# Where the low parts are subtracted: GpSimd or VectorE ahead of the attention

## The chip, the cores and the metric

The kernel runs on one core of one Trainium2 chip. The metric is the device time in microseconds of one execution: the median of three executions, with the lowest and the highest beside it. The profile below is one further execution, taken by the hardware profiler; its own time is given with it.

## What is computed

One layer of a diffusion backbone over 1024 latent tokens of width 1024, with 256 context tokens as a prefix, all in float32. Cut to what matters:

```
h, hc = modulate(x), modulate(ctx)                      # RMSNorm, then scale and shift from c
q, k, v, hy, gates = split(h @ w_in + b_in)             # 8 query heads, 2 key/value heads of 128
kc, vc = the k and v columns for the context tokens
attn = softmax(rope(norm(q)) @ [kc; rope(norm(k))]^T) @ [vc; v]
K    = rfft(filter MLP over positions)                  # 2 orders x 512 channels, length 2048
hy_o = two gated long convolutions of dwconv3(hy) by K  # each irfft(rfft(u) * K)
x   += g1 * ((sig(ga) * (attn @ w_attn) + sig(gh) * (hy_o @ w_hy)) @ w_o + b_o)
x   += g2 * ((gelu(a) * g) @ w_down + b_down),  [a, g] = dwconv3(modulate(x) @ w_up + b_up)
out  = rmsnorm(x)
```

## The kernel before

Every large product is made of three TensorE passes over float32r operands (`mm3`, L184 to L186). An operand X is split into a high part, which is X cast to float32r by ScalarE, and a low part, which is X minus the high part: one subtraction of 128x512 elements in most places, through the helper `sub` (L174). The low part is needed by the second or the third pass. `sub` takes an engine, VectorE (`V`) unless it is told GpSimd (`G`).

The work up to the attention runs in this order of the program. The times are those of the profiled execution.

- To about 51 us: the small filter network and the modulation vectors.
- 51 to 152 us: the context tokens and the latent tokens are normalised, transposed and split into `hTh`, `hTl` by `norm_in` (L574 to L598), in pairs of 128-row tiles; beside it the filters' transforms run as a background generator (`filters`, with `split`, L388, for its 16-point DFT outputs `X`).
- 152 to 354 us: six weight chunks of `w_in` give the Hyena streams (`proj_ch`, then `hy_post`), with the filters' transforms still in the background, and `other_tables` (L720 to L734) makes high and low parts of ten transform tables: a load into `traw`, a cast into `thi`, a subtraction into `tlo`, two stores. `traw`, `thi` and `tlo` have one buffer each, so a table's load waits for the subtraction of the table before.
- 354 to 759 us: six gate chunks and six q, k, v chunks alternate (`gate_chunk`, `qkv_chunk`), with both long convolutions in the background (`longconv`: a forward transform to `zp`, the product with the filter, an inverse transform to `vp`, then `idft16` on VectorE). The transform tables `ft` and `it` come by DMA. `norm_rope` normalises and rotates q and k, and TensorE transposes the result.
- 759 to 860 us: two more gate chunks beside the first scores; `parts` (L1015) splits v, k and q for the attention.

Each weight chunk comes through `load_w` (L486): four times a load of 128x512 into `raw` (3 buffers), a cast into `whi` (6 buffers, ScalarE), and a subtraction into `wlo` (6 buffers). A third `raw` tile is reused only when the subtraction that reads it is done; the load that reuses it stands in SyncE's queue, and in the same queue stand the loads of the transform tables behind it. A `whi` or `wlo` buffer is reused when TensorE has finished with it.

Five calls place the subtraction on GpSimd: `load_w` by default (`wlo`), every second pair in `norm_in` (`hTl`), slots 5 and 7 of the filters' `split` (`Xl`), `other_tables` (`tlo`), and three of the `parts` calls (two of `v`, one of `kT`). After the attention `load_w` serves `w_hy` and `w_attn` as well. GpSimd's other work in the whole kernel is the low parts of q, the normalisation of the attention output and sums of down-projection weights during the attention, and low parts for `w_o`.

Order: up to the FFN the order on each engine is made by the planner of the tile framework, which goes by the order of the program and by its own estimates of when operands are ready; each engine then works its queue in order. From the FFN on (`tc.manual_schedule`) the order is written out by hand.

Of the kernel before, what the change touches and what calls it, by code (L numbers as in the profile page):

```python
# [165 lines left out]
def build(tc, A, out, stop=99):  # L166
# [6 lines left out]
    def sub(out, a, b, eng=V):  # L173
        eng.tensor_tensor(out=out, in0=a, in1=b, op=ALU.subtract)  # L174
# [220 lines left out]
    def filters():  # L395
        for half in range(2):
            for order in range(2):
                for kind in range(2):
                    z = fp.tile([P, 8, 256], F32, name="z", tag="z")
                    c0 = order * 512 + half * 256  # L400
                    wh = fp.tile([P, 256], F32R, name="woh", tag="woh")
                    S.copy(out=wh, in_=wo[:, kind, c0:c0 + 256])
                    wl = fp.tile([P, 256], F32R, name="wol", tag="wol")
                    sub(wl, wo[:, kind, c0:c0 + 256], wh)
                    for a2 in range(4):
                        if order == kind == 0:
                            decs[a2] = fp.tile([P, 2, 256], F32, name="dec", tag=f"dec{a2}")
                            ld(out=decs[a2], in_=A["k_dec"][half][:, a2 * 512:a2 * 512 + 512].rearrange(
                                "p (a c) -> p a c", a=2))
                        ps = pfh.tile([P, 2, 256], F32, name="fh", tag="fh")  # L410
                        for k in range(2):
                            a = 2 * a2 + k
                            T.matmul(ps[:, k], hms[:, a * P:a * P + P], wh, start=True, stop=False)
                            T.matmul(ps[:, k], hms[:, a * P:a * P + P], wl, start=False, stop=True)
                        tt(z[:, 2 * a2:2 * a2 + 2], ps, decs[a2], ALU.mult)
                    if kind == 0:
                        skip = fp.tile([1, 256], F32, name="skip", tag="ks", bufs=2)
                        ld(out=skip, in_=A["rows"][3:4, c0:c0 + 256])
                        tt(z[0:1, 0], z[0:1, 0], skip, ALU.add)
                    yield  # L420
                    def forward(slot, Xh, Xl):
                        tb = fwd_tab(slot)
                        ps = pfk.tile([P, 2, 256], F32, name="fk", tag="fk")
                        if slot == 0:
                            m = (0, 1) if kind == 0 else (2, 3)
                        else:
                            m = (0, 1) if kind == 0 else (1, 0)
                        mm3(ps[:, 0], *tb[m[0]], Xh[:, 0], Xl[:, 0], True, False)
                        mm3(ps[:, 0], *tb[m[1]], Xh[:, 1], Xl[:, 1], False, True)
                        if slot == 0:  # L430
                            ks = fp.tile([P, 256], F32, name="ks", tag="ks", bufs=2)
                            S.copy(out=ks, in_=ps[:, 0])
                            if kind == 0:
                                (rh, rl) = tb[2]
                                mm3(ps[0:1, 1], rh[:, 0:1], rl[:, 0:1], Xh[:, 0], Xl[:, 0], True, True)
                                st(out=k_d[order, half, :, 0], in_=ks)
                                kd = fp.tile([P, 256], F32, name="ks", tag="ks", bufs=2)
                                S.copy(out=kd, in_=ps[:, 0])
                                S.copy(out=kd[0:1], in_=ps[0:1, 1])
                                st(out=k_d[order, half, :, 1], in_=kd)  # L440
                            else:
                                V.memset(ks[0:1], 0.0)
                                ld(out=k_d[order, half, :, 2], in_=ks)
                        else:
                            ks = fp.tile([P, 256], F32, name="ks", tag="ks", bufs=2)
                            S.copy(out=ks, in_=ps[:, 0])
                            st(out=k_d[order, half, :, 1 + 2 * slot + kind], in_=ks)

                    ahead = []
                    for slot, X in dft16(fp, z, 2, kind == 0):  # L450
                        ahead.append((slot, *split(fp, X, 2, "X", G if slot in (5, 7) else V)))
                        yield
                        if len(ahead) > 1:
                            forward(*ahead.pop(0))
                            yield
                    forward(*ahead.pop(0))
                    yield
# [25 lines left out]
    def raw_tile():  # L483
        return wp.tile([P, 512], F32, name="raw", tag="raw", bufs=3)

    def load_w(src, pool=None, eng=G, nraw=3, nhi=6):  # L486

        pl = pool or wp
        res = []
        for i in range(len(src) if isinstance(src, list) else src.shape[0]):  # L490
            if isinstance(src, list):
                raw = src[i]
            else:
                raw = pl.tile([P, 2, 256], F32, name="raw", tag="raw", bufs=nraw)
                ld(out=raw, in_=src[i].rearrange("p (k c) -> p k c", k=2))
            hi = pl.tile([P, 2, 256], F32R, name="whi", tag="whi", bufs=nhi)
            S.copy(out=hi, in_=raw)  # L497
            lo = pl.tile([P, 2, 256], F32R, name="wlo", tag="wlo", bufs=nhi)
            sub(lo, raw, hi, eng)
            for k in range(2):  # L500
                res.append((hi[:, k], lo[:, k]))
        return res
# [72 lines left out]
    def norm_in(xs, r, s, c0, late=False):  # L575

        for i in range(2):
            V.tensor_scalar(out=xs[i], in0=xs[i], scalar1=r[:, i:i + 1], scalar2=None, op0=ALU.mult)
        hh, hl, cs = hTh[c0 // 512], hTl[c0 // 512], slice(c0 % 512, c0 % 512 + 256)
        for c0_ in range(0, KT, 2):  # L580
            if late:
                ps = ptr.tile([P, 2, 256], F32, name="tr", tag="tr")
            elif c0_ % 4 == 0:
                ps = pmm.tile([P, 4, 256], F32, name="mm", tag="mm")
            n = ps.shape[1]
            hf = hfp.tile([P, 2, 256], F32, name="hf", tag="hf")
            for c in (c0_, c0_ + 1):
                for i in range(2):
                    T.transpose(ps[:, c % n, i * P:(i + 1) * P], xs[i][:, c * P:(c + 1) * P], ident)
            for j in range(2):  # L590
                c = c0_ + j
                a_, b_ = mod1[:, 8 + c, s:s + 1], mod1[:, c, s:s + 1]
                if j == 0:
                    S.activation(out=hf[:, j], in_=ps[:, c % n], func=AF.Identity, scale=a_, bias=b_)
                else:
                    V.tensor_scalar(out=hf[:, j], in0=ps[:, c % n], scalar1=a_, scalar2=b_, op0=ALU.mult, op1=ALU.add)
            S.copy(out=hh[:, c0_:c0_ + 2, cs], in_=hf)
            sub(hl[:, c0_:c0_ + 2, cs], hf, hh[:, c0_:c0_ + 2, cs], (G, V)[c0_ // 2 % 2])  # L598


    def qk_pool(n):
# [118 lines left out]
    def other_tables():  # L720
# [4 lines left out]
        for src, dst, n in inv_r:  # L725
            raw = hyp.tile([P, 512], F32, name="traw", tag="traw", bufs=1)[:, 0:n * P]
            ld(out=raw, in_=src)
            hi = hyp.tile([P, 512], F32R, name="thi", tag="thi", bufs=1)[:, 0:n * P]
            S.copy(out=hi, in_=raw)
            lo = hyp.tile([P, 512], F32R, name="tlo", tag="tlo", bufs=1)[:, 0:n * P]  # L730
            sub(lo, raw, hi, G)
            st(out=dst[:, 0], in_=B32(hi).rearrange("p (a b) -> p a b", b=P))
            ld(out=dst[:, 1], in_=B32(lo).rearrange("p (a b) -> p a b", b=P))
            yield  # L734
# [291 lines left out]
    def pt_tile(odd=1):  # L1026
        return (ap if odd else pte).tile([P, NKEY], F32, name="Pt", tag="Pt", bufs=4)
# [3 lines left out]
    parts(kT[0], kT_d[0], pt_tile())  # L1031
    for i in range(2):
        parts([v[:, 5 * i:5 * i + 5] for v in vv], v_d[:, 5 * i:5 * i + 5],
              pt_tile().rearrange("p (k d) -> p k d", d=256), G)
    parts(kT[1], kT_d[1], pt_tile(), G)
    KS = ((1024, 256), (0, 512), (512, 512))

    def scores(q, g, qt, sm, Pt):
# [201 lines left out]
        return ps  # L1240

    for ci in range(4):
        w = load_w(A["w_hy"][ci], wp, nraw=5) if ci else load_w([raw_hy[:, 0], raw_hy[:, 1]], wp, V, nraw=5)
        for m2 in range(2):
            m = 2 * ci + m2
            ps = branch(w, m2, 4, hyh, hyl)
# [12 lines left out]

    mix = [half_pair(0), half_pair(1)]  # L1260
    for ci in range(4):
        w = load_w(A["w_attn"][ci], wp, nraw=5)
        for m2 in range(2):
            m = 2 * ci + m2
            ps = branch(w, m2, 8, *[[o[:, :, 512 * h:512 * h + 512] for h in range(2)] for o in (oTh, oTl)])
# [608 lines left out]
```

## Time and profile before

| | |
|---|---|
| median of 3 executions | 2023.29 us (2020.77 to 2024.64) |
| profiled execution, its time | 2025.56 us |
| its span, first to last instruction | 2023.8 us |
| TensorE matmul busy | 1893.8 us, 94% |
| VectorE busy | 1545.9 us, 76% |
| ScalarE busy | 968.2 us, 48% |
| GpSimd busy | 422.0 us, 21% |

An engine's busy time is the union of its instructions' spans. Idle time before an instruction is put down to what released it, by semaphore events. The profile also tells the clock that TensorE was granted, as a share of its full speed. In the stretches of the change, 51 to 860 us, GpSimd has 155 instructions; from the end of the attention's neighbourhood on, the change touches nothing.

### The profile page before, as it was taken

What the parts mean: (1) busy time and instruction counts of PE and PEld (TensorE: products, weight loads), DVE (VectorE), ACT (ScalarE), POOL (GpSimd) and SP (SyncE); (2) the same over time, 40 slices, a digit from 0 to 9 for tenths busy, and PEclk for the clock granted to TensorE, in tenths of its full rate; (3) what the DMA queues carried; (4) which work ended last, traced back from release to release, by engine and by line L of the source; (5) the groups of instructions that cost most, each with busy time, mean ns of one, the idle gap of its engine ahead of it and who ended that gap; (6) DMA issues with size and microseconds to landing.
All of it is one profiled execution on the core that took longest, in us unless ns stands there. A gap on an engine that the chain in (4) does not pass through costs nothing.

```text
span 2023.8 us, 27726 instructions
## 1 busy us (share of the span) xinstructions
PE 1893.8 (94%) x9776; PEld 1570.5 (78%) x9776; DVE 1545.9 (76%) x2630; ACT 968.2 (48%) x1958; POOL 422.0 (21%) x270
## 2 busy tenths in 40 slices
PE   7789899889989989999999999998999999899997
PEld 1667778879878888788887777787888888678885
DVE  6987885896878633677776663889888888878788
ACT  3754443442444334687777332345444444445443
POOL 0553331222141231344532133440000000000000
PEclk8899999999999999999999999999999999999998
DMA  7435434747555331444434874742333333349762
GB/s 296 158 102 201 150 97 156 243 145 240 185 168 158 126 130 58 135 141 150 128 100 85 287 273 168 253 151 65 120 108 106 115 104 109 126 149 339 249 204 98
DMA packets 181131, 322.54 MB, mean 159 GB/s; under 512 B 26955, under 2 KB 65359, under 8 KB 180096
## 3 DMA queue, kind: packets, MB, share of 16 engines
q1 hardware_dynamic: 156256, 287.01, 43.7%
q10 hardware_dynamic: 24736, 33.76, 4.7%
q8 instruction: 77, 1.26, 0.3%
q14 instruction: 62, 0.51, 0.1%
HBM read 245.03 MB, written 75.68 MB: 158 GB/s over the span
## 4 chain that ended last, share of the span: by engine, by line
PE 57%; DVE 21%; DMA 6%; issue 5%; ACT 3%; POOL 2%; SPq 0%; ACTq 0%; DVEq 0%; POOLq 0%
PE mm L186 6%; PE mm L185 6%; PE mm L184 6%; PE b L184 5%; PE b L186 5%; PE b L185 5%; PE tp L1144 3%; DVE ua L180 2%; DVE ug L180 2%; PE s L184 2%; PE s L186 2%; PE s L185 2%; PE o L185 2%; PE o L186 2%; PE o L184 2%
## 5 line engine op out<-in xcount | busy, mean ns | idle before, releaser
L174 POOL TENSOR_TENSOR wlo<-raw,whi 128x512 fp32r<-128x512 f32 x138 | 234.2, 1709 | 601.1 <-ACT whi L497 499.1
L184 PE MATMUL mm<-hTh,whi 128*128 128x512 f32 x448 | 180.5, 403 | 2.6 <-ACT sg L973 1.4
L185 PE MATMUL mm<-hTl,whi 128*128 128x512 f32 x448 | 179.8, 401 | 0.5 <-DVE hTl L174 0.5
L186 PE MATMUL mm<-hTh,wlo 128*128 128x512 f32 x448 | 179.4, 400 | 0.0
L1046 DVE TENSOR_REDUCE mx<-s 128x1 f32<-128x512 f32 (+1 forms) x192 | 113.3, 598 | 58.7 <-PE s L186 57.0
L185 PE MATMUL mm<-wlo,hTh 128*128 128x256 f32 x416 | 118.8, 286 | 8.8 <-POOL wlo L174 8.4
L1051 ACT ACTIVATE Pt<-s,mx 128x512 f32<-128x512 f32 (+1 forms) x192 | 116.1, 614 | 20.2 <-DVE mx L1049 18.8
L186 PE MATMUL mm<-whi,hTl 128*128 128x256 f32 x416 | 118.6, 285 | 0.7 <-DVE hTl L174 0.5
L174 DVE TENSOR_TENSOR PTl<-tp,PTh 128x512 fp32r<-128x512 f32 x160 | 108.2, 685 | 13.7 <-ACT PTh L1146 10.3
L184 PE MATMUL mm<-whi,hTh 128*128 128x256 f32 x416 | 118.5, 285 | 0.0
L388 ACT CAST Xh<-X 128x512 fp32r<-128x512 f32 x128 | 78.0, 620 | 76.1 <-DVE X L177 35.6
L1146 ACT CAST PTh<-tp 128x512 fp32r<-128x512 f32 x160 | 92.7, 594 | 39.5 <-PE tp L1144 39.4
L186 PE MATMUL b<-bh,al 128*128 128x512 f32 x284 | 110.6, 390 | 0.6 <-DVE al L174 0.6
L184 PE MATMUL b<-bh,ah 128*128 128x512 f32 x284 | 110.6, 390 | 0.4 <-ACT ah L1731 0.4
L185 PE MATMUL b<-bl,ah 128*128 128x512 f32 x284 | 110.6, 389 | 0.0
L497 ACT CAST whi<-raw 128x512 fp32r<-128x512 f32 x110 | 66.5, 617 | 87.7 <-PE mm L185 41.2
L174 DVE TENSOR_TENSOR Xl<-X,Xh 128x512 fp32r<-128x512 f32 x112 | 80.6, 737 | 35.2 <-ACT Xh L388 35.0
L184 PEld LDWEIGHTS mm<-hTh,whi 128*128 128x128 f32 x448 | 85.9, 192 | 18.5 <-ACT sg L973 1.8
L186 PEld LDWEIGHTS mm<-hTh,wlo 128*128 128x128 f32 x448 | 86.2, 192 | 16.3
L185 PEld LDWEIGHTS mm<-hTl,whi 128*128 128x128 f32 x448 | 86.3, 193 | 16.0 <-DVE hTl L174 0.9
L1144 PEld LDWEIGHTS tp<-ident,Pt 128*128 128x128 f32 x640 | 77.3, 140 | 22.7 <-issue 3.7
L1144 PE MATMUL tp<-ident,Pt 128*128 128x128 f32 x640 | 93.8, 273 | 1.1 <-DVE PTl L174 0.8
(388 smaller groups left out, 5770.4 us busy)
## 6 DMA issues: line engine op xcount, KB each, us to landing
raw<-w_up SPq DMA_DIRECT2D x132, 256.0 KB, 2.8
raw<-w_in SPq DMA_DIRECT2D x88, 256.0 KB, 3.1
wm<-w_mod SPq DMA_DIRECT2D x64, 256.0 KB, 4.3
raw<-act_d SPq DMA_DIRECT2D x25, 512.0 KB, 3.3
wd<-w_down SPq DMA_DIRECT2D x44, 256.0 KB, 4.2
ws_d<-wd SPq DMA_DIRECT2D x44, 256.0 KB, 4.4
act_d<-ug SPq DMA_DIRECT2D x44, 256.0 KB, 2.2
ft<-fwd_d SPq DMA_DIRECT2D x28, 384.0 KB, 4.0
```

The lines of the kernel that those rows point to most:

```text
L174: eng.tensor_tensor(out=out, in0=a, in1=b, op=ALU.subtract)
L180: eng.scalar_tensor_tensor(out=out, in0=a, scalar=s, in1=b, op0=op0, op1=op1)
L184: T.matmul(o, lh, rh, start=start, stop=False, skip_group_check=more)
L185: T.matmul(o, lh, rl, start=False, stop=False, skip_group_check=more)
L186: last_mm[0] = T.matmul(o, ll, rh, start=False, stop=stop, skip_group_check=more)
L388: S.copy(out=h, in_=X)
L497: S.copy(out=hi, in_=raw)
L1046: V.tensor_reduce(out=mx[:, j:j + 1], in_=s[:, :n], axis=AX.X, op=ALU.max)
L1051: S.activation(out=Pt[:, o:o + n], in_=sps[j][:, :n], func=AF.Exp, bias=mx[:, 3:4], accum_out=sm[:, j:j + 1])
L1144: T.transpose(tp[:, i * P:i * P + P], cur[i][:, kt * P:kt * P + P], ident)
L1146: S.copy(out=th, in_=tp)
```

## The change

The default engine of `load_w` becomes VectorE, and the two callers after the attention (`w_hy`, `w_attn`) now name GpSimd, so that they stay as they were. The subtractions in `norm_in`, in the filters' `split`, in `other_tables` and in the three `parts` calls go to VectorE too. No buffer count, no cast and no DMA is changed. Ahead of the attention GpSimd keeps no subtraction but that of q (`load_q`).

```diff
@@ filters()
                     for slot, X in dft16(fp, z, 2, kind == 0):
-                        ahead.append((slot, *split(fp, X, 2, "X", G if slot in (5, 7) else V)))
+                        ahead.append((slot, *split(fp, X, 2)))
@@
-    def load_w(src, pool=None, eng=G, nraw=3, nhi=6):
+    def load_w(src, pool=None, eng=V, nraw=3, nhi=6):
@@ norm_in()
             S.copy(out=hh[:, c0_:c0_ + 2, cs], in_=hf)
-            sub(hl[:, c0_:c0_ + 2, cs], hf, hh[:, c0_:c0_ + 2, cs], (G, V)[c0_ // 2 % 2])
+            sub(hl[:, c0_:c0_ + 2, cs], hf, hh[:, c0_:c0_ + 2, cs])
@@ other_tables()
-            sub(lo, raw, hi, G)
+            sub(lo, raw, hi)
@@ v and k for the attention
     parts(kT[0], kT_d[0], pt_tile())
     for i in range(2):
         parts([v[:, 5 * i:5 * i + 5] for v in vv], v_d[:, 5 * i:5 * i + 5],
-              pt_tile().rearrange("p (k d) -> p k d", d=256), G)
-    parts(kT[1], kT_d[1], pt_tile(), G)
+              pt_tile().rearrange("p (k d) -> p k d", d=256))
+    parts(kT[1], kT_d[1], pt_tile())
@@ after the attention
-        w = load_w(A["w_hy"][ci], wp, nraw=5) if ci else load_w([raw_hy[:, 0], raw_hy[:, 1]], wp, V, nraw=5)
+        w = load_w(A["w_hy"][ci], wp, G, nraw=5) if ci else load_w([raw_hy[:, 0], raw_hy[:, 1]], wp, V, nraw=5)
@@
-        w = load_w(A["w_attn"][ci], wp, nraw=5)
+        w = load_w(A["w_attn"][ci], wp, G, nraw=5)
```

## Rows read from the trace of the kernel before

**Rows 1.** The page's first part: busy time, share of the span and instructions of engines.
```profile
PE 1893.8 (94%) x9776; PEld 1570.5 (78%) x9776; DVE 1545.9 (76%) x2630; ACT 968.2 (48%) x1958; POOL 422.0 (21%) x270
```

**Rows 2.** Busy time by stretch: stretch, its length, then engines as named.
```profile
51.00:152.00 101.00, 79.49 (x462) 64.87 (x461) 87.10 (x164) 66.05 (x140) 52.03 (x31) 0.94 0.40 130
152.00:354.00 202.00, 186.77 (x994) 153.39 (x993) 154.11 (x274) 90.52 (x175) 60.46 (x39) 0.98 0.46 151
354.00:506.00 152.00, 140.21 (x962) 131.00 (x961) 126.25 (x267) 57.14 (x132) 35.21 (x16) 0.97 0.65 209
506.00:607.00 101.00, 88.09 (x588) 81.68 (x587) 81.52 (x177) 40.56 (x104) 30.21 (x12) 0.95 0.56 176
607.00:759.00 152.00, 139.71 (x946) 129.09 (x945) 97.83 (x198) 62.35 (x191) 34.63 (x21) 0.96 0.44 138
759.00:860.00 101.00, 97.28 (x490) 80.30 (x489) 52.28 (x119) 59.11 (x149) 24.51 (x16) 0.98 0.30 97
```

**Rows 3.** GpSimd's groups by line and form, 51 to 860 us: busy, mean ns.
```profile
L174 POOL TENSOR_TENSOR wlo<-raw,whi 128x512 fp32r<-128x512 f32 x84 | 152.6, 1830 | 440.2 <-ACT whi L497 395.3 <-DMA it<-inv_d 44.1 <-issue 0.4
L174 POOL TENSOR_TENSOR Xl<-X,Xh 128x512 fp32r<-128x512 f32 x16 | 24.0, 1500 | 54.7 <-ACT Xh L388 50.5 <-DMA traw<-k_fwd 2.9 <-issue 1.2
L174 POOL TENSOR_TENSOR tlo<-traw,thi 128x512 fp32r<-128x512 f32 x9 | 17.8, 1978 | 24.4 <-ACT thi L729 12.4 <-PE fk L186 12.0
L174 POOL TENSOR_TENSOR hTl<-hf,hTh 128x512 fp32r<-128x512 f32 x10 | 15.7, 1574 | 17.6 <-ACT hTh L597 17.5
```

**Rows 4.** The tile Xl, VectorE's instructions, 51 to 860 us: ns min/median/max.
```profile
L174 DVE TENSOR_TENSOR Xl<-X,Xh x110: 616/682/1779, 61.5 to 661.7; 128x512 fp32r<-128x512 f32 x110
```

**Rows 5.** Timelines of VectorE: the first and the last lengthened instruction of 70.
```profile
57.42 0.64 DVE L177 TENSOR_TENSOR mod<-mod,vecs 128x8 f32<-128x8 f32 x1
...
765.46 1.40 DVE L174 TENSOR_TENSOR ropeA<-ropeA,ropeB 128x256 f32<-128x256 f32 x1
```

**Rows 6.** TensorE's waits, 51 to 860 us: us in total, times, longest.
```profile
PE tr L659 <- DVE ropeA L177: 12.3, 4, 5.4
PE fk L184 <- ACT Xh L388: 10.8, 3, 6.1
PE zp L184 <- ACT Xh L388: 9.2, 3, 4.1
PE mm L185 <- POOL wlo L174: 8.4, 1, 8.4
PE fk L185 <- DVE Xl L174: 7.7, 10, 2.0
PE zp L184 <- DMA ft<-fwd_d: 5.8, 3, 3.8
```

**Rows 7.** Waits of SyncE's queue, 51 to 860 us, in the same columns.
```profile
SPq L495 <- POOL wlo L174: 284.2, 73, 27.9
...
SPq L733 <- POOL tlo L174: 37.4, 9, 7.5
```

**Rows 8.** ScalarE's casts whi in 51 to 860 us, with the idle time before.
```profile
L497 ACT CAST whi<-raw 128x512 fp32r<-128x512 f32 x88 | 53.2, 618 | 67.2 <-PE mm L185 32.9 <-DMA raw<-w_in 21.7 <-issue 5.1
```

**Rows 9.** Timeline of GpSimd, 139 to 152 us: start, duration.
```profile
139.34 6.66 POOL L174 TENSOR_TENSOR tlo<-traw,thi 128x512 fp32r<-128x512 f32 x1 [1.11 <-ACT thi L729]
150.26 1.28 POOL L174 TENSOR_TENSOR tlo<-traw,thi 128x512 fp32r<-128x512 f32 x1 [4.26 <-ACT thi L729]
```

**Rows 10.** Timeline of ScalarE near 150 us.
```profile
149.57 0.62 ACT L729 CAST thi<-traw 128x512 fp32r<-128x512 f32 x1 [8.13 <-DMA traw<-k_inv]
150.09 0.61 ACT L388 CAST Xh<-X 128x512 fp32r<-128x512 f32 x1
```

**Rows 11.** Timeline of GpSimd from 586.6 us.
```profile
586.70 13.37 POOL L174 TENSOR_TENSOR wlo<-raw,whi 128x512 fp32r<-128x512 f32 x1 [18.91 <-ACT whi L497]
```

**Rows 12.** Timelines of VectorE and GpSimd from 698 us.
```profile
698.36 1.77 DVE L177 TENSOR_TENSOR ropeB<-qr,rope 128x512 f32<-128x512 f32 x1
700.17 1.37 DVE L174 TENSOR_TENSOR ropeA<-ropeA,ropeB 128x256 f32<-128x256 f32 x1
701.46 1.48 DVE L177 TENSOR_TENSOR ropeA<-ropeA,ropeB 128x256 f32<-128x256 f32 x1
...
698.31 4.35 POOL L174 TENSOR_TENSOR wlo<-raw,whi 128x512 fp32r<-128x512 f32 x3 [19.81 <-ACT whi L497]
```

**Rows 13.** Busy time by stretch, columns as in rows 2; three stretches of lower clock.
```profile
149.40:156.20 6.80, 5.44 (x18) 4.75 (x19) 4.15 (x6) 2.03 (x4) 1.28 (x1) 0.50 0.36 117
596.50:603.30 6.80, 3.18 (x15) 3.18 (x16) 2.44 (x8) 0.59 (x2) 6.04 (x3) 0.50 0.24 72
702.30:709.10 6.80, 6.01 (x17) 4.87 (x18) 3.37 (x10) 5.14 (x24) 0.36 (x1) 0.50 0.58 176
```

## The prediction, made before the changed kernel was run

> **What bounds the kernel now.** I read the page's busy times first: TensorE is busy 94% of the span, VectorE 76%, GpSimd 21% [rows 1]. So only TensorE's idle time and its time at the lower clock can be won. Next the busy time by stretch, from 51 us to 860 us, where every edit lies [rows 2]: TensorE's six numbers sum to 731.6 of 809 us, so 77 us are idle there, and no edit can win much more. VectorE is not full but close: 0.86 of the first stretch, 0.76, 0.83, 0.81 and 0.64 of the next four. The waits of TensorE tell what it misses [rows 6]: once GpSimd's wlo itself (8.4 us), and otherwise what hangs on VectorE, on ScalarE or on a load: the rotated q and k (12.3), the casts Xh (10.8 and 9.2), Xl (7.7), the tables ft (5.8). That is 54 us of the 77. So the question is how far GpSimd's subtractions cause those other waits.
>
> They do so in two ways. **VectorE and GpSimd exclude each other.** A subtraction of 128x512 on GpSimd takes 1.28 us where nothing disturbs it [rows 9] and 1.50 to 1.98 us in the mean [rows 3]; one lasted 6.66 us [rows 9] and one 13.37 us [rows 11]. VectorE's same subtraction takes 0.682 us in the median and 1.779 at most [rows 4]. From 698 us, three short VectorE instructions of a rotation take 1.77, 1.37 and 1.48 us while GpSimd works on wlo [rows 12]. Counting every VectorE instruction between 51 and 860 us that is over 0.2 us longer than the lower quartile of its own line, tiles and shape, I find 70, which carry 70.8 us of excess; the first and the last are in [rows 5]. By stretch of rows 2 the excess is 17.8, 21.2, 7.6, 4.6, 18.5 and 1.0 us. **GpSimd holds queues.** SyncE's queue waits 284.2 us for wlo before it may load the next raw tile, and 37.4 us for tlo [rows 7]; the table loads stand behind. Most of the 284 is only the wait for TensorE to free whi, but each stretched subtraction adds to it.
>
> **The change part by part. Removed** from GpSimd are 84 wlo, 16 Xl, 10 hTl, 10 tlo (nine in the row, one shorter) [rows 3], two v and one kT of 1280 columns. **Added** to VectorE are the same 123. For 120 of them I take 0.682 us [rows 4], 82 us; for the three long ones 2.5 times that at most, 1.7 us each, 5 us. VectorE gets 87 us and loses up to 70.8 us of excess: 16 us net. By stretch, with GpSimd's counts of rows 2 (31, 39, 16, 12, 19 moved): 21 against 17.8; 27 against 21.2; 11 against 7.6; 8 against 4.6; 13 plus the long ones against 18.5. VectorE's busy share would go from 0.86 to 0.90 in the first stretch, from 0.76 to 0.79 in the second, and fall in the fifth.
>
> Now the waits of TensorE, one by one. (a) At 150.8 us: tlo took 6.66 us, the next table's load waited for its buffer, ScalarE stood 8.13 us at the cast of that table, and Xh was queued behind it [rows 9, 10]; TensorE waited 6.1 [rows 6]. On VectorE, tlo lasts 0.7, so the load goes out some 5 us sooner: gain 5, between 3 and 6. What is late next is Xl, 0.7 us behind Xh. (b) The wait of 8.4 us for wlo, which lasted 13.37 [rows 6, 11]. The four lows of a chunk cost VectorE 2.7 us, so the gain is 5.6 to 8.4; I take 7. (c) The table loads ft, 5.8 us: the raw loads ahead of them in SyncE's queue waited for stretched wlo. I take 4, between 1 and 5.8. (d) The rotations, 12.3 us in four waits. Each is lengthened by about 3.1 us where three GpSimd lows stand beside it [rows 12]; if the planner puts three VectorE lows, 2.0 us, in the same place, 1 us each is won, otherwise 3. I take 5, between 4 and 12. (e) zp for Xh, 9.2 us in three, behind the inverse DFT on VectorE, by the same arithmetic: 3, between 1 and 6. (f) The filters' waits in the first two stretches (the rest of fk for Xh, 10.8 less 6.1, and Xl, 7.7): here VectorE's net work grows by 9 us. If all of it lies on the path 9 us are lost; if the excess lay on the path and the lows do not, some 4 are won. I take a loss of 3. (g) The clock. After a long idle stretch the granted clock is 0.50, that is 1.2 of 2.4 GHz: 5.44 us of work at 150 us, 3.18 at 597, 6.01 at 702 [rows 13]. Half of such busy time comes back where the stall goes: 2.7 + 1.6 for (a) and (b), and about half of 3.0 for (d) twice, 3: 7 in all with nothing taken for (c) and (e); between 3 and 11.
>
> (h) **New waits.** VectorE works in order, so a low now stands in front of what is queued behind it when its whi is late: the DFTs, the rotations, and by those Xh, ropeA and TensorE. ScalarE, in order too, waits 67.2 us ahead of its whi casts [rows 8], 32.9 of it for TensorE to free a buffer and 21.7 for raw. No row shows VectorE waiting for whi, so I bound it: 0, if the planner leaves room or VectorE would idle anyway (in the stretches from 354 to 860 us it idles 148 of 506 us, rows 2), and 34, half of ScalarE's waits. I take 8: nearest is (a), where one such wait of ScalarE of 8.13 us reached TensorE with 6.1. Costed at nothing: the three long parts, from 740 us on, beside gate matmuls in a stretch where VectorE is busy half the time; without that cover 5 us. The stores of tlo stay where they are in SyncE's queue and go sooner. GpSimd's own queue holds no DMA here.
>
> The sum: 5 + 7 + 4 + 5 + 3 − 3 + 7 − 8 = 20 us of gain. The profiled execution took 2025.6 us (span 2023.8 and 1.8 around it), 2.3 above the median 2023.3; less 20 it gives 2005.6, and against the median **2003 us**, −1.0%. With all good ends the gain is 6 + 8.4 + 5.8 + 12 + 6 + 4 + 11 = 53; with all bad ends it is 3 + 5.6 + 1 + 4 + 1 − 9 + 3 − 34 = −25.
>
> One rule is worth weighing. The row shows a wlo of 13.37 us [rows 11] while VectorE runs without a break, and GpSimd gets through only when VectorE stops. The Trainium skill, "SBUF — State Buffer", section "Who interferes with whom", says that the two engines share one port pair and that whichever issues first holds it for its whole instruction, the other blocking. Read as a turn for each instruction, one wlo could lose no more than one VectorE instruction, and (b) would win about nothing: 13 instead of 20 us, 2010. The row speaks for the stronger form, that GpSimd loses every turn.
>
> **The rivals.** *The lows take the place of the excess.* The planner puts each low where GpSimd's stood, VectorE is as late as before, and only (a) and (b) are won with their clock: 5 + 7 + 4 = 16 us, against which VectorE's 16 us of net work falls on the path for 9 and (h) costs 8: 2024, no change. For it speaks that VectorE's busy shares hardly fall; against it that a long GpSimd subtraction delays three instructions at unlucky moments, while an ordered queue lets the planner choose. *VectorE's queue is held by late whi, the slower side.* Place: the chunk borders, where the last two whi of a chunk wait for TensorE to free a buffer. Price: 34 us (h) and 9 us (f), against 5 + 7 + 4 + 5 + 3 + 7 = 31 won: 12 us slower, 2035. It decides from 28 us of new waits that reach TensorE. For it speak ScalarE's 67.2 us [rows 8] and that GpSimd idled 440 us at just this place [rows 3], which cost nothing on a free engine; against it that much of VectorE's next work hangs on ScalarE's next cast anyway. *VectorE becomes full.* The Trainium skill, "Perfetto Trace Analysis", section "Optimizing Scalar/DVE Operations", says that work may be taken off a full VectorE, though to GpSimd, with the shared port, it may not help. As a mechanism of this kernel: if the excess of the first stretch is not given back, its 31 lows cost 21 us instead of 3, VectorE is full (87.1 + 21 of 101 us), and 18 of the 20 us are gone: 2021. *The change does not do what it says:* if the 70 long instructions have another cause, VectorE gets 87 us, its waits grow, and it ends as the slower rival; the short rotation rows beside GpSimd speak against it.
>
> **How the numbers follow.** Forecast 0.57, 1988 to 2016 by its own unknowns. Given back 0.16, at 2018 to 2028. Late whi 0.17, with the last rival in it, at 2028 to 2045. VectorE full 0.10, at 2016 to 2025. What a measurement can tell from no change is about 0.2%, 4 us: faster means under 2019.2. Faster is the forecast, less a little, 0.55, with 0.03 of the given-back and 0.06 of the full case: 0.64. Within: 0.16. Slower: 0.20. The range 1988 to 2032 leaves out about 0.1 on top and 0.1 below.
>
> **What would show it.** Right: no VectorE instruction but a few above 0.2 us over its quartile between 51 and 740 us; VectorE's busy time there up by 10 to 20 us; no wait of TensorE for wlo over 3 us; no ScalarE wait over 5 us ahead of thi; TensorE's idle time of 51 to 860 us from 77 down to some 60. Wrong: VectorE idle ahead of wlo for whi by over 20 us in sum, or new waits of TensorE for Xl and ropeA. Since the planner makes the order anew, waits may also move to places that no row shows; that is the largest thing I cannot price.

## The result and the profile after

The changed kernel takes **1975.6 us** in the median of five (1970.98 to 1976.68), against 2023.29; the ratio is 0.9759, with a 95% interval of 0.9748 to 0.977. The forecast was 2003 in a range of 1988 to 2032: the direction was right, the gain was 48 us where 20 were forecast, and the time lies below the range. (GpSimd's 155 instructions between 51 and 860 us, as told ahead of the prediction, are 135 by the counts of [rows 2].)

The page's first part, of the changed kernel (it answers to [rows 1]):

```profile
PE 1880.5 (95%) x9776; PEld 1564.1 (79%) x9776; DVE 1547.4 (78%) x2753; ACT 968.0 (49%) x1958; POOL 201.8 (10%) x147
```

VectorE has 123 instructions more and is busy for 1.5 us more, not for 16. TensorE does the same 9776 matmuls in 13.4 us less, and its granted clock over the span is 0.980 against 0.975. To see where the rest went, both traces are cut at the same pieces of work: at the last low part of h, at the end of the last filter product `fk`, at the first low part of the attention's P, and at the end. Busy time by stretch, first of the kernel before and then of the changed one (columns: stretch, length, TensorE, its weight loads, VectorE, ScalarE, GpSimd, granted clock, share and rate of DMA):

```profile
0.00:123.80 123.80, 98.19 (x441) 57.31 (x442) 101.48 (x206) 69.01 (x142) 35.71 (x28) 0.92 0.57 197
123.80:329.00 205.20, 185.05 (x997) 152.11 (x996) 167.97 (x297) 96.82 (x188) 73.32 (x45) 0.98 0.42 140
329.00:819.60 490.60, 449.05 (x2860) 408.14 (x2858) 332.99 (x695) 194.66 (x508) 111.93 (x58) 0.96 0.51 164
819.60:2023.80 1204.20, 1161.56 (x5481) 952.96 (x5481) 943.45 (x1433) 607.69 (x1122) 201.01 (x141) 0.99 0.48 157
```

```profile
0.00:109.60 109.60, 92.60 (x427) 54.75 (x427) 91.07 (x206) 65.69 (x133) 0.70 (x6) 0.94 0.63 220
109.60:300.10 190.50, 183.99 (x1024) 155.01 (x1023) 178.12 (x365) 101.16 (x197) 0.00 (x0) 0.99 0.45 152
300.10:768.90 468.80, 440.75 (x2848) 399.86 (x2846) 335.99 (x752) 193.70 (x507) 0.44 (x1) 0.97 0.54 172
768.90:1974.90 1206.00, 1163.12 (x5481) 954.45 (x5481) 942.22 (x1433) 607.42 (x1122) 200.70 (x141) 0.98 0.48 157
```

The three stages up to the attention are 14.2, 14.7 and 21.8 us shorter; what follows is the same within 2 us. (Background work moves a little between the first two: TensorE has 441 and 997 matmuls there before, 427 and 1024 after.) In these three, VectorE's busy time is the same to 3 us (602.4 and 605.2), and its idle time falls from 217 to 164. TensorE's idle time falls from 87.3 to 51.6: 35.8 us of idle time and 14.9 of matmul time make the 50.7 us of these stages. VectorE's share rose all the same, as the same work stands in a shorter stretch: of the 101 us from 51 us on it works 96.8, against 87.1 before, and TensorE 92.5 against 79.5 [rows 2]:

```profile
51.00:152.00 101.00, 92.47 (x546) 78.43 (x546) 96.79 (x216) 71.41 (x150) 0.00 (x0) 0.95 0.40 129
```

TensorE's waits from 51 to 815 us in the changed kernel, in the columns of [rows 6]; lines in between are left out:

```profile
PE zp L184 <- ACT Xh L388: 8.9, 4, 5.3
PE mm L185 <- DVE wlo L174: 7.0, 2, 6.8
PE mm L186 <- DVE wlo L174: 3.1, 1, 3.1
PE fk L184 <- ACT Xh L388: 2.9, 4, 1.8
...
PE fk L185 <- DVE Xl L174: 2.5, 4, 1.3
PE mm L184 <- DVE hf L596: 1.9, 2, 1.0
...
PE zp L184 <- DMA ft<-fwd_d: 1.7, 2, 0.8
...
PE tr L659 <- DVE ropeA L177: 0.2, 1, 0.2
```

In the kernel before, the same view has, among others, these four lines on the first two stages, which [rows 6] leave out:

```profile
PE tr L589 <- DVE hf L596: 4.0, 3, 2.2
...
PE fk L185 <- POOL Xl L174: 2.0, 4, 0.9
...
PE mm L184 <- DVE hf L596: 1.2, 1, 1.2
...
PE mm L589 <- DVE hf L596: 0.6, 1, 0.6
```

The waits of the rotations (12.3 us before) are gone but for 0.2, those of fk for Xh fall from 10.8 to 2.9, of Xl from 7.7 to 2.5, of the tables ft from 5.8 to 1.7. The wait for wlo did not go: 8.4 us on GpSimd became 10.1 on VectorE. The timeline of VectorE shows why, with two of the lows of one chunk and what follows the first; under it ScalarE's cast for the second low, and TensorE's first matmul after:

```profile
626.27 0.68 DVE L174 TENSOR_TENSOR wlo<-raw,whi 128x512 fp32r<-128x512 f32 x1
626.87 1.75 DVE L174 TENSOR_TENSOR Vt<-Vt 128x1536 f32<-128x1536 f32 x1
...
640.07 0.68 DVE L174 TENSOR_TENSOR wlo<-raw,whi 128x512 fp32r<-128x512 f32 x1
```

```profile
626.49 0.62 ACT L497 CAST whi<-raw 128x512 fp32r<-128x512 f32 x1 [0.74 <-PE mm L185]
640.80 0.58 PE L185 MATMUL mm<-wlo,hTh 128*128 128x256 f32 x1 [6.85 <-DVE wlo L174]
```

The planner put the second low behind the whole inverse DFT, 13 us of VectorE's work without a gap, though its whi was cast by 627.1 us, and TensorE waited 6.85 us for it. Before, GpSimd was shut out by the same DFT [rows 11].

VectorE's lengthened instructions, counted against the lower quartile of the changed kernel's own durations, are 70 with 70.9 us before the attention in the kernel before, and none in the changed kernel.

### The profile page after: what moved, and what is told of

Its sections match the earlier page's. It is cut to its first block, busy times and chain, and to the rows that moved or that the text cites. A ratio compares the mean times of both kernels' runs of the same rounds, so it can differ in the third digit from the quotient of the medians.

```text
span 1974.9 us, 27638 instructions
## 1 busy us (share of the span) xinstructions
PE 1880.5 (95%) x9776; PEld 1564.1 (79%) x9776; DVE 1547.4 (78%) x2753; ACT 968.0 (49%) x1958; POOL 201.8 (10%) x147
## 4 chain that ended last, share of the span: by engine, by line
PE 60%; DVE 21%; DMA 5%; issue 5%; ACT 4%; SPq 0%; POOL 0%; ACTq 0%; DVEq 0%; POOLq 0%
PE mm L186 7%; PE mm L185 7%; PE mm L184 7%; PE b L184 5%; PE b L186 5%; PE b L185 5%; PE tp L1144 3%; DVE ua L180 2%; DVE ug L180 2%; PE s L184 2%; PE s L186 2%; PE s L185 2%; PE o L185 2%; PE o L186 2%; PE o L184 2%
## 5 line engine op out<-in xcount | busy, mean ns | idle before, releaser
L174 DVE TENSOR_TENSOR wlo<-raw,whi 128x512 fp32r<-128x512 f32 x158 | 106.8, 688 | 46.6 <-ACT whi L1512 31.8
L1051 ACT ACTIVATE Pt<-s,mx 128x512 f32<-128x512 f32 (+1 forms) x192 | 116.1, 615 | 17.8 <-DVE mx L1049 16.3
L184 PE MATMUL b<-bh,ah 128*128 128x512 f32 x284 | 110.6, 390 | 0.2 <-ACT ah L1731 0.2
L185 PE MATMUL b<-bl,ah 128*128 128x512 f32 x284 | 110.6, 389 | 0.0
L174 DVE TENSOR_TENSOR Xl<-X,Xh 128x512 fp32r<-128x512 f32 x128 | 85.0, 683 | 19.5 <-ACT Xh L388 19.1
L174 POOL TENSOR_TENSOR qT<-qf,qT 128x1024 fp32r<-128x1024 f32 x7 | 16.7, 2392 | 809.7 <-DMA sg_d<-sg 767.2
L174 POOL TENSOR_TENSOR wlo<-raw,whi 128x512 fp32r<-128x512 f32 x54 | 81.3, 1518 | 160.5 <-ACT whi L497 101.7
L185 PEld LDWEIGHTS mm<-hTl,whi 128*128 128x128 f32 x448 | 84.7, 189 | 14.8
```

Of the source, the lines that this page charges most:

```text
L184: T.matmul(o, lh, rh, start=start, stop=False, skip_group_check=more)
L185: T.matmul(o, lh, rl, start=False, stop=False, skip_group_check=more)
L1051: S.activation(out=Pt[:, o:o + n], in_=sps[j][:, :n], func=AF.Exp, bias=mx[:, 3:4], accum_out=sm[:, j:j + 1])
```

## Experiments

Times are medians; ratios are to runs of the kernel before on the same chip, with their 95% intervals. Spans are of the one profiled execution. The runs stand on several chips, where the kernel before has medians of 2023.3 to 2029.3 us, so spans of different chips compare to some 5 us only; where it matters the ratios are given beside them. "Excess" is the sum by which VectorE's instructions ahead of the attention exceed their durations in the changed kernel, counted where it is over 0.2 us.

### GpSimd's reads alone

Beside each low that is now formed by VectorE, GpSimd works too, for nobody:

```diff
+    scr = gp.tile([P, 2, 256], float8, name="scr")
+    shadow = lambda hi: G.tensor_tensor(out=scr, in0=hi, in1=hi, op=ALU.subtract)
...
-            sub(lo, raw, hi, eng)
+            sub(lo, raw, hi, eng); shadow(hi)        # in load_w; in norm_in for every second pair
```

In the built program TensorE, VectorE, ScalarE and SyncE have the very order of the changed kernel. The trace counts 98 extra instructions, not 94: the four lows of the second context chunk, which VectorE had before, got one too.

> The changed kernel with 94 extra GpSimd subtractions ahead of the attention, one for each wlo (of load_w) and for every second hTl. Each reads the high part twice and writes a scratch tile that nobody reads; the order on TensorE, VectorE, ScalarE and SyncE is that of the changed kernel. Its result is still the reference's. Exclusion theory (GpSimd's reads lengthen VectorE's instructions, and that was the cost): some 45 to 65 us of excess come back on VectorE, and 25 to 45 of the 48 us gained are lost: 2000 to 2020 us. Latency theory (the low part itself came late, and held raw tiles and queues): nobody waits for the extra work and no raw tile is held, so at most a few us are lost: under 1985. Order theory (the planner's new order brought the gain): the order is the same, under 1985.

Measured: 2015.4 us, ratio 0.9955 (0.9938 to 0.9972). The span is 38.8 us over the changed kernel's, with 50.3 us of excess in 69 instructions. The same order, with GpSimd reading beside it, gives back four fifths of the gain. In its trace no engine waits for `scr`, and no instruction of ScalarE is over 0.2 us longer than in the changed kernel, so neither the order nor anyone's wait for GpSimd is needed for that. The tile view of `scr` (ns min/median/max):

```profile
L213 POOL TENSOR_TENSOR scr<-whi x88: 1041/1368/16515, 52.1 to 772.3; 128x512 fp8e4<-128x512 f32 x88
```

One took 16.5 us; its line, and one of VectorE's near its end:

```profile
579.62 16.52 POOL L213 TENSOR_TENSOR scr<-whi 128x512 fp8e4<-128x512 f32 x1 [18.91 <-ACT whi L497]
595.23 0.69 DVE L177 TENSOR_TENSOR X<-zp,kt 128x512 f32<-128x512 f32 x1
```

VectorE worked without a gap all the while, on instructions with two operands in SBUF, and went on after. GpSimd was done 0.9 us after the first that reads one of its two operands, zp, from PSUM. VectorE and GpSimd shut each other out, and in such a run of VectorE's instructions GpSimd loses every turn.

> As the run before with two extra subtractions for each, 188 in all, same order elsewhere. Exclusion theory: the loss is between 1.5 and 2 times that of 94. Latency or order theory: still under 1990 us.

Measured: 2068.7 us, ratio 1.0221 (1.0202 to 1.0239); the span is 90.8 us over the changed kernel's, 2.3 times the loss of the single dose, with 110.6 us of excess (the trace's instructions are 196, twice 98). Loss for each us of excess: 0.77 and 0.82.

### The same extra work on VectorE

```diff
-    shadow = lambda hi: G.tensor_tensor(out=scr, in0=hi, in1=hi, op=ALU.subtract)
+    shadow = lambda hi: V.tensor_tensor(out=scr, in0=hi, in1=hi, op=ALU.subtract)
```

> The changed kernel with the same 98 extra subtractions as in shadow_out (88 beside wlo, 10 beside hTl, into the scratch tile), now on VectorE, some 0.68 us each, 67 us of added VectorE work; the order is the planner's. Theory A (a us of lengthening at a moment that GpSimd picks costs nearly a us of the end, 38.8 us for 50.3 of excess in shadow_out, while a us of work in VectorE's own queue is mostly put into its idle time): under 15 us lost against the changed kernel, below 1990 us. Theory B (my sum: excess and added work count alike, VectorE's total decides): 67 us of work cost more than the 50 us of excess did: 2015 us or more.

Measured: 2002.8 us, ratio 0.9881 (0.9856 to 0.9907); the span is 24.7 us over the changed kernel's. That is between the two theories: 67 us of VectorE's instructions cost 0.37 us each us, half the price of excess. Nearly all of it is lost by the end of the filters, 20.7 us (320.8 us from the start against 300.1). (The planner ordered this kernel anew.) The same 98 subtractions cost 38.8 us on GpSimd, where nobody waits for them, and 24.7 on VectorE, which was thought to be the loaded engine.

### Without the lows

```diff
+        skip = eng is V and pool is None
...
-            lo = pl.tile([P, 2, 256], F32R, name="wlo", tag="wlo", bufs=nhi)
-            sub(lo, raw, hi, eng)
+            lo = hi if skip else pl.tile(...)         # and sub only if not skip; no_low_shadow: shadow(hi) on GpSimd if skip
```

and in the same way for Xl of slots 5 and 7 and for tlo.

> The changed kernel without 110 of the low parts: the 84 wlo, the 16 Xl and the 10 tlo are left out and the high part is read in their place (the hTl, v and kT stay on VectorE), so 75 us of VectorE work are gone and nothing stands on GpSimd. What the lows cost where they stand is the difference. If VectorE's own work costs little until it is full (a third of a us each): 25 us under the changed kernel, 1950, so that the kernel before pays 75 us. If it costs 0.7 us each, as in the first two stages of the run with 98 more on VectorE: 50 us, 1925. If the lows fit into idle time: under 10 us, 1966 or more.

> As the run before, with 110 GpSimd subtractions that read the high parts and write a scratch tile nobody reads: GpSimd's work of the kernel before without anybody waiting for it. The difference to the run without it is the exclusion alone, the difference from it to the kernel before is what late lows and held raw tiles cost. Exclusion theory: the larger part, 45 to 60 us above the run before (some 60 to 75 us of excess), and 10 to 25 us below the kernel before. If lateness and held tiles were the larger part: under 30 us above.

Measured: 1949.6 us, ratio 0.9601 (0.9572 to 0.9629), and with GpSimd's shadow 1972.6, ratio 0.9707 (0.9676 to 0.9739). The spans are 1946.2 and 1971.8. So, in spans:

| the 110 lows | span | over none |
|---|---|---|
| left out | 1946.2 | |
| on VectorE (the changed kernel) | 1974.9 | 28.7 |
| on GpSimd, read by nobody | 1971.8 | 25.6 |
| on GpSimd, and waited for (the kernel before) | 2023.8 | 77.6 |

(The kernel before also has ten hTl, two v and one kT there, which all other rows have on VectorE.) The first expectation holds at a third of a us: 75 us of lows cost 28.7 us, 0.38 for each. By the ratios they cost 32 us, 0.43 for each. The second falls: GpSimd's work for nobody costs 25.6 us with 36.7 us of excess, not 45 to 60 (by the medians, both of one chip, 23.0, which is 0.63 for each us of excess against 0.70). It is not all exclusion, as one cast does wait for these reads, that of the tables, whose `thi` has a single buffer:

```profile
ACT thi L736 <- POOL scr L738: 11.3, 5, 4.0
```

The larger part of what the kernel before paid, 52 us (57 by the medians), comes only when lows are waited for and hold raw tiles and tables. These 52 us have more excess in them (71 against 37), so they are not all waiting: at 0.6 to 0.85 us each the 34 us of excess would be, as an estimate, 20 to 29 of them, and the rest, 23 to 37, late lows, held buffers and order. The planner ordered each of these kernels anew (no_low and no_low_shadow differ in 131 of 9776 places on TensorE), and what the order does is not separated here.

### Late lows without GpSimd

```diff
-            sub(hl[:, c0_:c0_ + 2, cs], hf, hh[:, c0_:c0_ + 2, cs])
+            sub(hf, hf, hh[:, c0_:c0_ + 2, cs])       # every second pair; so too for Xl and tlo
+            S.copy(out=hl[:, c0_:c0_ + 2, cs], in_=hf)
```

> The changed kernel with 36 lows made late without GpSimd: for every second hTl, for Xl of slots 5 and 7 and for tlo VectorE subtracts in place (over hf, X, traw) and ScalarE copies the result into the low part, which is so some 0.65 us and a turn in ScalarE's queue later, with the source held as long as GpSimd held it; 36 copies are 22 us of added ScalarE work. No exclusion takes place. If lateness and held buffers of these 36 were a large share of what the first two stages lost: 15 us or more lost against the changed kernel before 350 us (1990 or more). If exclusion and order were nearly all: under 6 us lost (under 1982).

Measured: 1985.3 us, ratio 0.9794 (0.9776 to 0.9813), 6 us over the changed kernel on the same chip (1979.3); in the traces the filters end 309.6 us from the start instead of 300.1 (301.0 on the same chip), and a part of that is made up afterwards. At the end that is the edge of the second theory, "under 6 us"; up to the filters' end, 9 us lie between the two. So 36 lows that are 0.65 us late cost 6 us in all, with ScalarE's 22 us of added copies in it; late wlo were not tried. What GpSimd cost in lateness beyond that came, it seems, of the stretched lows, 6.66 and 13.37 us [rows 9, 11], and those stand beside runs of VectorE's work; no run isolates them.

### One part alone

Each is one line of the change put into the kernel before.

> The kernel before with the wlo of load_w alone on VectorE up to the attention (84 of the 123 subtractions); hTl, Xl, tlo, v and kT stay on GpSimd. By counts of the exclusion theory 84 of 123, about two thirds: 33 us won, 1990 us, most of it after 354 us. If the tables' tlo and the hTl are what holds the first two stages, less: 1998 to 2005, with nothing won before 350 us.

> The changed kernel with the wlo of load_w put back on GpSimd: hTl, Xl, tlo, v and kT alone on VectorE (39 subtractions). Exclusion theory by counts: 15 us won, 2008 us. If tlo and hTl hold the first two stages: 25 us or more, under 2000, won before 350 us.

> The kernel before with the ten tlo of the transform tables alone on VectorE. My step (a): 5 us and 2.7 of clock, 2016 us, all between 124 and 330 us. By counts of the exclusion theory 10 of 123, with nothing for the chain of loads: 4 us, 2020.

> The kernel before with the 16 Xl of slots 5 and 7 alone on VectorE. TensorE waited 2 us for them on GpSimd, so by waits 2 us; by counts of the exclusion theory 6 us; if the filter transforms are one serial chain (DFT, cast, low, matmul) on which GpSimd's 1.5 us instead of 0.7 counts twice per transform, 8 transforms, up to 13 us: 2011 us.

> The kernel before with the ten hTl of norm_in alone on VectorE. By counts of the exclusion theory 10 of 123: 4 us. If the first stage is held by them, the stage from 51 us to the last hTl is 5 us or more shorter and the whole 5 us or more. The replanned order alone moves stages by some us as in the runs with one part moved, so under 4 us says nothing.

| on VectorE | lows | median us | ratio (95%) | span, to before |
|---|---|---|---|---|
| wlo | 84 | 2001.9 | 0.989 (0.9869 to 0.9911) | −24.0 |
| all but wlo | 39 | 1998.8 | 0.9876 (0.9851 to 0.99) | −30.4 |
| tlo | 10 | 2019.8 | 0.9952 (0.9935 to 0.9969) | −2.0 |
| Xl of slots 5, 7 | 16 | 2023.7 | 0.9985 (0.9967 to 1.0002) | −8.6 |
| hTl | 10 | 2032.8 | 1.0023 (1.001 to 1.0037) | +0.3 |

The 84 wlo won 24 us (23 by the medians), under the 33 of the count; the time lies in the second expectation's range, though 8 us were won by the end of the filters, where it expected nothing. The 39 others won 30 (26 by the medians), as much as the second expectation said, and 25 of it by the end of the filters. These two halves add up to the whole gain. But tlo, Xl and hTl alone add up to some 8 us by the medians and 10 by the spans. With tlo alone the median is 8.1 us lower, as step (a) said with its 7.7; in the profiled execution, one of the slowest of ten, the filters end 9.6 us sooner, and 7.6 of these are lost again after them, where the built program's order is that of before. Xl's interval includes no change. hTl alone won nothing, against both expectations. So the small parts don't add up; that one removed leaves the others to hold the same stretch is a guess that no run tests. The excess left is 23.2 us with wlo moved and 47.2 with all but wlo, of 70.9. Up to the end of the filters both kernels lose nearly the same excess (39.2 us before, 16.3 and 17.2 left) and put nearly as many lows on VectorE (31 wlo; 36 hTl, Xl and tlo), yet the first wins 7.9 us there and the second 24.7. So in the first two stages the netting of excess and lows isn't what decides; what these 36 lows make others wait for, or the order, is.

### More of the same

```diff
-        w = load_w(A["w_attn"][ci], wp, G, nraw=5)
+        w = load_w(A["w_attn"][ci], wp, V, nraw=5)    # w_hy too, and w_o's halves; more_V2: and m0l
```

> The changed kernel with the wlo of w_hy, w_attn and w_o on VectorE too, so that after the attention GpSimd keeps four subtractions. VectorE loses most of the 26 us of excess there and gains 38 us of work. If a us of excess costs 0.8 us wherever it is: 15 to 20 us won, 1957. If it costs only where TensorE waits for VectorE: TensorE waits some 10 us in all in that part, so at most 5 us either way, 1970 to 1980.

> The changed kernel with the wlo of w_hy, w_attn and w_o and the low parts of the FFN's first input tiles (m0l) on VectorE, so that GpSimd works only beside the attention. If the 5 us of the run without m0l hold: 1967 to 1972 us, 3 to 6 us under the changed kernel of this chip, won before the last product of w_o.

> The changed kernel once more, on the chip of the two runs with more on VectorE: 1971 to 1977 us.

Measured: 1970.2 us, ratio 0.9717 (0.9694 to 0.974), then with m0l 1972.5, ratio 0.9731 (0.9712 to 0.9749), beside the changed kernel on the chip of the second at 1979.3, ratio 0.9762 (0.9741 to 0.9783), a little over what was expected of it. These two are the best versions found, 7 us under the changed kernel on the second's chip and 9 by the ratio of the first; their intervals overlap. Nearly all the 26 us of excess after the attention are gone (3.1 and 0.7 are left), and only 5 to 9 us came of it; a price of 0.8 us for each us does not hold in a part where TensorE hardly waits for VectorE.

## Why the prediction was wrong

**Right:** the two ways in which GpSimd costs (mutual exclusion, and held queues), the 70 instructions and their 71 us, and that all of it goes. Of its own signs two failed: VectorE's busy time up to the attention rose by 2.8 us, not by 10 to 20, and TensorE waited 6.8 and 3.1 us for wlo where no wait was to be over 3. Of the steps, by TensorE's waits before and after:

| step | forecast us | measured us |
|---|---|---|
| (a) fk for Xh behind the tables | 5 | 6.1 |
| (b) wlo at chunk borders, and (h) new waits | 7 − 8 = −1 | 8.4 to 10.1: −1.7 |
| (c) the tables ft | 4 | 5.8 to 1.7: 4.1 |
| (d) rotations | 5 | 12.3 to 0.2: 12.1 |
| (e) zp for Xh | 3 | 9.2 to 8.9: 0.3 |
| (f) the filters and h, first two stages | −3 | the rest of Xh 4.7 to 2.9, 7.7 to 2.5 for Xl, 2.0 to 0 for GpSimd's Xl, 5.8 to 2.4 for hf: 12.4 |
| (g) the clock | 7 | 13.4 |

(The clock's row is the matmul time of the whole program. hf, which the forecast did not name, is 4.0 + 1.2 + 0.6 before, 1.9 and a line of 0.5 after.) The measured waits sum to 33.3 us; the rest of the 35.8 us of idle time lies in smaller waits.

**The step that failed is (f)**, and the arithmetic under it: "VectorE gets 87 us and loses up to 70.8 us of excess: 16 us net". That made the two a common currency and gave the first two stages, where VectorE's load would rise, a loss of 3 us. Those stages won 28.9, and TensorE's waits named here fell by 12.4.

The runs show two things in its place. First, over the whole program the two have different prices. A us of lengthening cost 0.63 to 0.85 us of the end (no_low_shadow, shadow_out, shadow_out2, by spans or by ratios); a us of VectorE's own subtractions cost 0.38 to 0.43 (no_low) and 0.37 (shadow_V). That is at most about half of the gain: as an estimate, 70.9 us of excess at these prices are 45 to 60 us, and 87 us of lows cost 32 to 37, which leaves 7 to 28 of the 49 us.

The difference arises after the filters: from there to the attention the extra subtractions cost 3.9 us on VectorE and 18.0 on GpSimd.

Second, in the stages of (f) the two engines hardly differ. Up to the end of the filters the extra subtractions for nobody cost 20.7 us on VectorE (shadow_V) and 22.8 on GpSimd (shadow_out); the lows cost 7.5 on VectorE (300.1 us against 292.6 in no_low), and GpSimd's work for nobody 9.1 (301.7). What those stages won comes where GpSimd's lows are waited for (329.0), and mostly with hTl, Xl and tlo (24.7 us, against 7.9 with wlo). Step (f) had no term for that: it counted these lows as load on VectorE and not as late or as holding their buffers; only (a) did, for one table. 36 such lows late by 0.65 us cost 9 us by there (late_low). How far late lows, held buffers and the planner's new order share the rest stays open.

**VectorE's 16 us net were not there.** Its busy time rose by 1.5 us. The durations of [rows 4] overlap at their ends: in the changed kernel's timeline above the next instruction starts 0.60 us after a low that is told as 0.68. A sum of told durations overstates a queue by an eighth, here by some 10 of the 87 us. (By 0.60 us each, the lows of no_low and shadow_V cost 0.42 to 0.49 for each us; the gap to the price of excess is narrower, and stays.)

**(d)** was mis-sized at 5 for 12.1: I kept two of the three us of each rotation for lows that would stand in the same place; the planner put at most one there (one at 670.93 us, told as 0.66, just ahead of the two last instructions of a rotation), and TensorE waited 0.2 us in all. **(g)** was mis-sized at 7 for 13.4, as its half shares were taken of (a), (b) and (d) alone; over the whole program the granted clock rose from 0.975 to 0.980. That it rose because the waits of (d) and (f) went is likely, but not shown.

**(b) and (h)** came out as forecast in sum, by luck of two errors: the wait for wlo was not won, and no other new wait of TensorE is over 1.2 us. ScalarE's wait of 8.13 us ahead of a table's cast [rows 10] is now 4.0 at most. VectorE waits for whi 14.8 us in eight, under the 20 that was to be the sign of being wrong; the 8 I took were of TensorE's time, and TensorE's new waits have other causes.

**The rivals.** "Late whi" appeared in small, at its place (a chunk border) but by VectorE's own work rather than by whi, at 6.85 us and not 34. "VectorE becomes full" came as a share (0.96 of 51 to 152 us, over the 0.90 of the forecast) but not as a cost, and "the lows take the place of the excess" did not come. The Trainium skill's rule on the port pair ("SBUF — State Buffer", "Who interferes with whom") holds as to who contends; read as one lost turn for each instruction it does not: 16.5 us for one GpSimd subtraction [shadow_out's tile view] is some 35 VectorE instructions long. By that reading (b) would have won nothing; it won nothing, but because the low stands behind the same run in VectorE's own queue.

**Still open:** how the 52 us that only waited-for GpSimd lows cost are shared between late results, held buffers, the order and the extra excess, and why tlo, Xl and hTl alone bring a third of what they bring together (with v and kT). 36 lows late by 0.65 us (late_low) cost 6 us at the end; what the raw tiles held by wlo cost [rows 7] was not measured by itself.

## What to carry to other kernels

Work that one engine inflicts on another's queue and work that the engine plans itself have different prices: here 0.63 to 0.85 against some 0.4 us for each us, as a mean over stages that differ. Do not net them in one sum; and where others wait for the moved work, price that wait and the buffers held by it in a term of its own: in the first two stages the moved work cost nearly the same on either engine as long as nobody waited for it. Where an engine looks loaded, ask first how much of its idle time is waiting for others that wait for it. An engine that "costs nothing" because nobody waits for its results can still cost 23 to 40 us; a run with that work added, for nobody and in an unchanged order, measures it directly. See in its trace that nobody waits for the added work.

## What was not expected of the hardware

GpSimd's subtraction does not alternate with VectorE's instructions of two SBUF operands but waits until a run of them ends: 6.66, 13.37 and, with the shadow, 16.5 us for an instruction of 1.04 to 1.28 us. The 13.37 ended once VectorE stopped; the 6.66 and the 16.5 ended while VectorE worked on, within 1.2 us of the start of an instruction that reads one operand from PSUM (u<-mm at 144.80 us, X<-zp at 595.23). VectorE, on the other side, is held by 0.73 us in the mean, 0.86 at most in shadow_out (50.3 us in 69 instructions), less than one GpSimd instruction.
